# Tile 3 gathered instead of tile 6, and top-k scans taken into the query projections

## The chip, the cores and the metric

The kernel runs on one core of a Trainium2 chip. The metric is the device time of one execution in microseconds; a kernel's time is the median of its runs. TensorE (PE in the profile) multiplies matrices, VectorE is DVE, ScalarE is ACT, GpSimd is POOL, and SP is the queue that issues most transfers.

## The reference

One encoder layer on 1024 tokens of width 1024: a projection, forgetting attention (FoX) and RWKV-7 time mixing side by side, a gated merge, a layer norm, then PEER, a lookup of single-neuron experts, and a second layer norm. The change concerns PEER:

```python
q = (xb @ w_q).reshape(t, PEER_HEADS, 2, PEER_HALF)
s = jnp.einsum('thpd,hpkd->thpk', q, sub_keys).astype(jnp.float32)
top_s, top_i = lax.top_k(s, K)
cand_s = top_s[:, :, 0, :, None] + top_s[:, :, 1, None, :]
cand_i = top_i[:, :, 0, :, None] * PEER_N_KEYS + top_i[:, :, 1, None, :]
best_s, best_pos = lax.top_k(cand_s.reshape(t, PEER_HEADS, K * K), K)
idx = jnp.take_along_axis(cand_i.reshape(t, PEER_HEADS, K * K), best_pos, axis=-1)
gate = jax.nn.softmax(best_s, axis=-1).astype(xb.dtype)
h = jax.nn.gelu(jnp.einsum('thkd,td->thk', u_table[idx], xb), approximate=False)
return jnp.einsum('thk,thkd->td', gate * h, v_table[idx])
```

There are 8 heads with two sets of 128 sub-keys each (16 key sets), K is 16, so every token has 128 experts out of 16384. `u_table` and `v_table` are 16384 x 1024 float32.

## The kernel before

Tokens are cut into eight tiles of 128. The front works in two halves of 512 tokens (tiles 0 to 3, then 4 to 7): `fox`, `rwkv_half`, `merge_half`, and at the end of the merge `queries`, which computes the 16 projections and the scores of four tiles. Scores of four key sets at a time (a group) leave PSUM by an ACT copy and go to a DRAM tensor `scd`.

After the second half `dense_block` treats PEER in two ways. For the three tiles in `DENSE` (3, 4, 5) it computes the hidden values of all 16384 experts by matmul, in a loop of 128 steps of 128 experts over all of `u` and `v`; the gates enter through coefficients C, which a one-hot stage of 96 steps before the loop builds from each tile's selected indices (two one-hot matrices a token, multiplied on TensorE; part of C stays in SBUF, part goes to DRAM as `cd` and comes back). The five tiles in `GATHERED` (0, 1, 2, 6, 7) fetch only their chosen rows: 128 key rows a tile (one row of `u` for each of the 128 tokens, 128 x 1024 float32), by an indirect DMA on GpSimd and a product with a sum on VectorE (`experts_in`), and then 128 value rows a tile from `v`, by indirect DMA and small matmuls (`Rows`, tile `pg`; a step takes two rows).

Two background queues run beside the main code. `g.B` holds generators of top-ks (`topk`) and key rows (`experts_in`); `g.V` holds the value rows. Every matmul issued by `mm` pays both queues its priced length in us times a rate (`RATEP` by stage of the front, fox, RWKV, merge with queries; `RATEB` and `RATEV` in the one-hot stage and in the loop), and a queue runs steps until its credit is spent. Each `yield` names the step's cost: 1.46 for a key row, 0.5 for half a key set of a scan, 3 for a value step. While one queue runs, matmuls pay it nothing. `mix` interleaves two generators by weights (`TKW`). A generator that yields None has nothing to do yet and gives its credit up.

`topk` waits until its tile's scores are all written, reloads them group by group, scans each key set (five VectorE operations: the largest eight, replaced, the next eight, and two index searches), adds candidates, scans those, and turns ranks into expert indices with one-hot products. Its results go to DRAM (`seld`, `cijd`, `gated`).

The order of `g.B` before: the top-k of tile 0; the rows of tiles 0, 1 and 2, each mixed with the top-k of the next tile; the top-ks of 4, 5 and 6; the rows of 6 mixed with the top-k of 7; the rows of 7. So when the one-hot stage begins, tile 3 has long been selected (`selections` asks for it with `need`), and the value rows start at the same time.

In the front only TensorE's order is that of the program; in `dense_block` also those of GpSimd and VectorE, so there an instruction that waits holds up all behind it on its engine. Key rows land in places of 128 x 1024: five in the first half, two more in the second (`KRING`), parts of C in the loop. The value rows have a ring of seven and the parts of C not yet written.

Of the kernel before, what the change touches and what calls it, by code (L numbers as in the profile page):

```python
# [22 lines left out]
LATER = 0  # L23
BLEAD = 3
KRING = (5, 2)
TKW = (45.0, 56.25, 59.895)
TKI = 1
RATEP = (1, 1, 0.9)

RATEB = (2.1, 0.46)  # L30
RATEV = (4.2, 0.52, 1.25)
SEL = (1, 2, 3)
DENSE = (3, 4, 5)
GATHERED = (0, 1, 2, 6, 7)
LATE = (4, 5, 6)

RING = 7

# [362 lines left out]
def body(ctx, g):  # L401
# [34 lines left out]

    g.rank = g.tk.tile([128, 16, 16], BF16, name="rank")
    dve.tensor_copy(g.rank, g.iota[:, 0:16, None].to_broadcast([128, 16, 16]))
    g.scored = set()
    g.B.add(topk(g, 0), "k0")  # L440
    for k, t in enumerate(SEL):
        g.B.add(mix(experts_in(g, k), 190.0, g.B.tagged(topk(g, t), f"k{t}"), TKW[k]), f"g{k}")
    for t in LATE:
        g.B.add(topk(g, t), f"k{t}")
    g.B.add(mix(experts_in(g, 6), 190.0, g.B.tagged(topk(g, 7), "k7"), TKW[2]), "g6")
    g.B.add(experts_in(g, 7), "g7")
    if g.stop:
        g.B.q = []

# [66 lines left out]
def front_setup(g, fe, order):  # L516
    tc, nc, A = g.tc, g.nc, g.A
    dve, act, sp = g.dve, g.act, g.sp
    fp = fe.enter_context(tc.tile_pool(name="fe", bufs=1))
    g.wp = fe.enter_context(tc.tile_pool(name="wp", bufs=1))  # L520
    g.W = Weights(g, order, len(order) // len(PARTS))
    tab = fp.tile([128, TAB.shape[1]], F32, name="tab")

    def tb(name, rows=slice(0, 128)):
        o, n = TAB_OFF[name]
        return tab[rows, o:o + n]

    g.tb = tb
    yield
    sp.dma_start(tab, A["tab"])  # L530
    g.rst = fp.tile([128, 512], BF16, name="rst")
    dve.memset(g.rst, 1.0)
    dve.memset(g.rst.rearrange("p (c t) -> p c t", t=64)[:, :, 0:1], 0.0)
    g.vec = vec = fp.tile([128, N_VEC], F32, name="vec")
    sp.dma_start(vec, A["vec"])
    g.omu = fp.tile([128, 14], F32, name="omu")
    dve.tensor_scalar(g.omu, vec[:, V_MU:V_MU + 14], -1.0, 1.0, op0=OP.mult, op1=OP.add)

    g.oka = fp.tile([128, 4], F32, name="oka")
    dve.tensor_scalar(g.oka, vec[:, V_KA:V_KA + 4], -1.0, 1.0, op0=OP.mult, op1=OP.add)  # L540
    g.prev = fp.tile([128, 14], F32, name="prev")
    dve.memset(g.prev, 0.0)
    g.sigma = fp.tile([128, 4, 2, 64], F32, name="sigma")
    dve.memset(g.sigma, 0.0)
    g.ck = fp.tile([128, T], F32R, name="ck")
    dve.memset(g.ck.bitcast(F32), 0.0)
    g.ccar = fp.tile([8, 1], F32, name="ccar")
    dve.memset(g.ccar, 0.0)
    yield


def fox(g, hf, X):
# [7 lines left out]
    with ExitStack() as fx:  # L560
# [98 lines left out]
        def chunks(ct, e, P_, yu, su, vc):  # L659
# [32 lines left out]
            if e:  # L692
                dve.reciprocal(su, su)
                pr = psT.tile([128, n], F32, name="pt")
                for qi in range(nq):
                    pe.transpose(pr[0:2, qi * 128:(qi + 1) * 128], su[:, qi, :], ident)
                ri = sm.tile([2, n], F32, name="ri", bufs=1)
                act.copy(ri, pr[0:2, :])
                yield
                pr = psT.tile([128, n], F32, name="pt")  # L700
                mm(g, pr, tb("sel2", slice(0, 2)), ri, True, True)
                dve.tensor_mul(yu, yu, pr)
                act.dma_start(g.yfd[ct * 128:(ct + 1) * 128, cols], yu)
                yield
# [550 lines left out]
def queries(g, hf, x1, rest, ps_):  # L1255
# [5 lines left out]
    with ExitStack() as fx:  # L1261
# [13 lines left out]
        def scores(gr, q):  # L1275
            for tt in range(n // 128):
                ps = ps_.tile([128, 4, 128], F32, name=f"o{tt}", bufs=2)
                for j in range(4):
                    mm(g, ps[:, j, :], q[:, j, tt * 128:(tt + 1) * 128], sk[:, 4 * gr + j, :], True, True)
                sc = qp.tile([128, 512], F32, name="sc", bufs=2)  # L1280
                act.copy(sc, ps.rearrange("p a b -> p (a b)"))
                sp.dma_start(g.scd[tt0 + tt][:, gr * 512:(gr + 1) * 512], sc)

        last = None
        for gr in range(4):
# [16 lines left out]
            g.scored.add(tt0 + tt)  # L1302


def topk(g, tile_):

    dve, act, sp = g.dve, g.act, g.sp
    while tile_ not in g.scored:
        yield None
    P = g.tk  # L1310
    tv = P.tile([128, 16, 16], F32, name="tv")
    ti = P.tile([128, 16, 16], U32, name="ti")
    def load(gr):
        sc = P.tile([128, 4, 128], F32, name="s", bufs=2)
        sp.dma_start(sc, g.scd[tile_][:, gr * 512:(gr + 1) * 512].rearrange("p (a b) -> p a b", a=4))
        return sc

    nxt = load(0)
    yield 1.0
    yield 1.0  # L1320
    for gr in range(4):
        sc = nxt
        if gr < 3:
            nxt = load(gr + 1)
        for j in range(0, 4, TKI):
            ii = range(4 * gr + j, 4 * gr + j + TKI)
            tmp = P.tile([128, 2, 128], F32, name="tmp")
            for i in ii:
                dve.max(tv[:, i, 0:8], sc[:, i % 4, :])
            for i in ii:  # L1330
                dve.match_replace(tmp[:, i % 2, :], tv[:, i, 0:8], sc[:, i % 4, :], NEG)
            for i in ii:
                dve.max(tv[:, i, 8:16], tmp[:, i % 2, :])
            yield 0.5 * TKI
            for i in ii:
                dve.max_index(ti[:, i, 0:8], tv[:, i, 0:8], sc[:, i % 4, :])
            for i in ii:
                dve.max_index(ti[:, i, 8:16], tv[:, i, 8:16], tmp[:, i % 2, :])
            yield 0.5 * TKI
    v4 = tv.rearrange("p (h s) k -> p h s k", s=2)  # L1340
    cand = P.tile([128, 8, NCAND], F32, name="cand")
    for a_, (n, o) in enumerate(zip(CAND, CAND_OFF)):
# [110 lines left out]
def dense_block(g, C):  # L1453
# [59 lines left out]
        return a, b  # L1513

    g.B.rate, g.V.rate = RATEB[0], RATEV[0]
    zx = ExitStack()
    xt = None
    n4 = n // 4
# [374 lines left out]
```

## Time and profile before

| | us |
|---|---|
| median of 3 runs | 3609.86 |
| lowest, highest run | 3596.46, 3627.01 |
| the profiled execution | 3587.89 |
| its span, first to last instruction | 3586.1 |
| mean granted TensorE clock | 0.938 |

The profile is of one execution. Times in it are us from the first instruction. A group or a stretch lists the busy time of an engine with the number of its instructions in brackets; the clock is the share of TensorE's full clock that was granted, and the DMA share is the mean busy share of the core's 16 DMA engines. A wait is put down to what ended it.

### The profile page before, as it was taken

What the parts mean: (1) busy time and instruction counts of PE and PEld (TensorE: products, weight loads), DVE (VectorE), ACT (ScalarE), POOL (GpSimd) and SP (SyncE); (2) the same over time, 40 slices, a digit from 0 to 9 for tenths busy, and PEclk for the clock granted to TensorE, in tenths of its full rate; (3) what the DMA queues carried; (4) which work ended last, traced back from release to release, by engine and by line L of the source; (5) the groups of instructions that cost most, each with busy time, mean ns of one, the idle gap of its engine ahead of it and who ended that gap; (6) DMA issues with size and microseconds to landing.
All of it is one profiled execution on the core that took longest, in us unless ns stands there. A gap on an engine that the chain in (4) does not pass through costs nothing. (4 is left out here: it accounts for less than half of the span.)

```text
span 3586.1 us, 55687 instructions
## 1 busy us (share of the span) xinstructions
PE 3156.2 (88%) x20656; PEld 2304.5 (64%) x20656; DVE 2263.6 (63%) x5118; ACT 1165.6 (33%) x2453; POOL 2071.5 (58%) x1686
## 2 busy tenths in 40 slices
PE   7899998999987778878767777999999999999997
PEld 5577776775566566557533323887777777776665
DVE  2235423359988997886478854777766767763324
ACT  3443222333432121201244433334333433333332
POOL 2032114415565565644365566888887888886773
PEclk9999998999998988899888888999999999999998
DMA  6373257878888888999698999999999999999995
GB/s 234 112 246 116 95 180 246 294 282 299 298 342 310 288 295 322 357 363 392 248 376 341 351 369 380 363 361 358 383 396 372 403 374 398 399 382 341 389 394 191
DMA packets 369377, 1133.15 MB, mean 316 GB/s; under 512 B 49744, under 2 KB 88400, under 8 KB 367312
## 3 DMA queue, kind: packets, MB, share of 16 engines
q0 software_dynamic: 184320, 671.17, 49.1%
q1 hardware_dynamic: 172672, 437.64, 33.8%
q10 hardware_dynamic: 12112, 20.78, 1.6%
q8 instruction: 162, 2.65, 0.3%
q14 instruction: 111, 0.91, 0.1%
HBM read 999.87 MB, written 129.56 MB: 315 GB/s over the span
## 5 line engine op out<-in xcount | busy, mean ns | idle before, releaser
L1429 POOL DMA_INDIRECT g<-u,eidx x566 | 696.9, 1231 | 448.3 <-DVE hh L1435 156.8
L1435 DVE CUSTOM_DVE_ANT_0 g<-g,ext 128x1024 f32<-128x1024 f32 x566 | 728.5, 1297 | 70.3 <-DMA g<-u,eidx 64.3
L1731 POOL DMA_INDIRECT vr<-v,ve x434 | 457.8, 1055 | 196.3 <-issue 104.1
L291 POOL TENSOR_TENSOR wl<-wraw,wh 128x1024 fp32r<-128x1024 f32 x65 | 157.1, 2416 | 439.9 <-ACT wh L290 334.3
L273 PE MATMUL pg<-vr,win 128*32 128x512 f32 x1736 | 311.9, 636 | 65.4 <-DMA vr<-v,ve 62.3
L273 PE MATMUL b<-xh,uh 128*128 128x384 f32 x1024 | 350.7, 342 | 14.2 <-DVE C L1616 13.0
L273 PE MATMUL b<-xh,ul 128*128 128x384 f32 x1024 | 352.2, 344 | 8.0 <-POOL ul L291 7.9
L273 PE MATMUL b<-xl,uh 128*128 128x384 f32 x1024 | 349.5, 341 | 0.0
L273 PE MATMUL v<-vl,ch 128*128 128x512 f32 x768 | 305.9, 398 | 12.8 <-POOL vl L291 12.7
L273 PE MATMUL v<-vh,ch 128*128 128x512 f32 x768 | 302.9, 394 | 0.0
L273 PE MATMUL v<-vh,cl 128*128 128x512 f32 x768 | 301.7, 393 | 0.0
L273 PE MATMUL pj<-xh,wh 128*128 128x512 f32 x624 | 281.9, 452 | 19.2 <-ACT xh L290 7.6
L290 ACT CAST uh<-uraw 128x512 fp32r<-128x512 f32 x256 | 158.6, 620 | 365.2 <-PE b L273 267.5
L1731 POOL DMA_INDIRECT C<-v,ve x206 | 215.0, 1044 | 90.2 <-issue 47.4
L273 PE MATMUL pj<-xl,wh 128*128 128x512 f32 x624 | 257.0, 412 | 1.9 <-DVE xl L291 1.9
L273 PE MATMUL pj<-xh,wl 128*128 128x512 f32 x624 | 255.7, 410 | 0.0
L291 DVE TENSOR_TENSOR vl<-vraw,vh 128x512 fp32r<-128x512 f32 x128 | 134.6, 1051 | 178.3 <-ACT vh L290 110.9
L290 ACT CAST vh<-vraw 128x512 fp32r<-128x512 f32 x256 | 158.2, 620 | 252.2 <-PE v L273 174.9
L273 PEld LDWEIGHTS v<-ab 128*128 128x128 f32 x768 | 112.1, 216 | 182.6 <-issue 107.4
L291 POOL TENSOR_TENSOR ul<-uraw,uh 128x512 fp32r<-128x512 f32 x128 | 171.3, 1338 | 88.6 <-ACT uh L290 73.3
L273 PEld LDWEIGHTS b<-xh,uh 128*128 128x128 f32 x1024 | 194.3, 190 | 35.1 <-DVE C L1616 15.5
L273 PEld LDWEIGHTS b<-xh,ul 128*128 128x128 f32 x1024 | 194.3, 190 | 34.9 <-issue 24.3
(357 smaller groups left out, 6598.0 us busy)
## 6 DMA issues: line engine op xcount, KB each, us to landing
uraw<-ut SPq DMA_DIRECT2D x128, 512.0 KB
vraw<-vt SPq DMA_DIRECT2D x128, 512.0 KB
wraw<-w SPq DMA_DIRECT2D x75, 512.0 KB
wh<-whd SPq DMA_DIRECT2D x75, 512.0 KB
wl<-whd SPq DMA_DIRECT2D x75, 512.0 KB
whd<-wh SPq DMA_DIRECT2D x71, 512.0 KB
whd<-wl SPq DMA_DIRECT2D x71, 512.0 KB
cd<-S SPq DMA_DIRECT2D x12, 1344.0 KB
```

What stands on the lines that cost most here:

```text
L273: g.pe.matmul(o, l, r, start=start, stop=stop_)
L290: g.act.copy(hi, src)
L291: (lo_eng or g.dve).tensor_sub(lo, src, hi.bitcast(F32))
L1429: pool.indirect_dma_start(out=place, out_offset=None, in_=A["u"], in_offset=bass.IndirectOffsetOnAxis(ap=idx[:, n:n + 1], axis=0))
L1435: dve.tensor_tensor_reduce(out=gg, in0=gg, in1=xt, scale=1.0, scalar=0.0, op0=OP.mult, op1=OP.add, accum_out=hh[:, k:k + 1])
L1731: g.pool.indirect_dma_start(out=place, out_offset=None, in_=g.A["v"], in_offset=bass.IndirectOffsetOnAxis(ap=self.meta[i][1][:, t:t + 1], ...
```

## The change

Tile 3 moves from `DENSE` to `GATHERED` and tile 6 the other way. The rows of tile 3 stand last in the front's queue, mixed with scans of three score groups. A new function `scans` takes scores that are still in SBUF and scans them without a reload: in the first half all four groups of tile 0 and three groups each of tiles 1 and 2 (ten scans, kept in key places, which are free then), in the second half three groups of tile 4, the first dense tile. These groups are not written to `scd`, and `topk` begins behind them. At the start of `dense_block` a new loop steps the top-k of tile 4 to its end, two background steps for each value step, before any one-hot work. Then the rest of tile 3's rows is mixed with the top-ks of 5, 6 and 7 at weights 1 to 2, followed by the rows of tile 7. The rates change. A small tile `ri` in `fox` shares the buffers of `th`.

```diff
-TKW = (45.0, 56.25, 59.895)
+TKW = (31.0, 38.8, 56.25)
+EARLY = (0, 1, 2)
 TKI = 1
-RATEP = (1, 1, 0.9)
-
-RATEB = (2.1, 0.46)
-RATEV = (4.2, 0.52, 1.25)
+RATEP = (1, 1, 1.15)
+
+RATEB = (2.1, 0.32)
+RATEV = (3.5, 0.555, 0.88)
 SEL = (1, 2, 3)
-DENSE = (3, 4, 5)
-GATHERED = (0, 1, 2, 6, 7)
-LATE = (4, 5, 6)
+DENSE = (4, 5, 6)
+GATHERED = (0, 1, 2, 3, 7)
...
-    g.scored = set()
+    g.scored, g.fresh, g.tops = set(), [], {}
+    g.B.add(scans(g, 3 * len(EARLY) + 1))
     g.B.add(topk(g, 0), "k0")
     for k, t in enumerate(SEL):
         g.B.add(mix(experts_in(g, k), 190.0, g.B.tagged(topk(g, t), f"k{t}"), TKW[k]), f"g{k}")
-    for t in LATE:
-        g.B.add(topk(g, t), f"k{t}")
-    g.B.add(mix(experts_in(g, 6), 190.0, g.B.tagged(topk(g, 7), "k7"), TKW[2]), "g6")
-    g.B.add(experts_in(g, 7), "g7")
+    g.B.add(mix(g.B.tagged(experts_in(g, 3), "g3"), 1.0, scans(g, 3), 1.0), "s3")
...
-                ri = sm.tile([2, n], F32, name="ri", bufs=1)
+                ri = sm.tile([128, n], F32, name="th", bufs=4)[0:2, :]
...
-                sc = qp.tile([128, 512], F32, name="sc", bufs=2)
+                if hf == 0:
+                    near = tt in EARLY and (gr < 3 or tt == 0)
+                    k = (3 * gr + tt) % 9 if near else 9 if gr < 3 or tt == 1 else tt - 1
+                    sc = g.keys.all[k // 2][:, k % 2 * 512:k % 2 * 512 + 512]
+                else:
+                    near = tt0 + tt == DENSE[0] and gr < 3
+                    sc = qp.tile([128, 512], F32, name="sf", bufs=3) if near else qp.tile([128, 512], F32, name="sc", bufs=4)
                 act.copy(sc, ps.rearrange("p a b -> p (a b)"))
-                sp.dma_start(g.scd[tt0 + tt][:, gr * 512:(gr + 1) * 512], sc)
+                if near:
+                    g.fresh.append((tt0 + tt, gr, sc.rearrange("p (a b) -> p a b", a=4)))
+                else:
+                    sp.dma_start(g.scd[tt0 + tt][:, gr * 512:(gr + 1) * 512], sc)
...
+def scan(g, tv, ti, gr, sc):
+
+    dve = g.dve
+    for i in range(4 * gr, 4 * gr + 4):
+        tmp = g.tk.tile([128, 2, 128], F32, name="tmp")[:, i % 2, :]
+        dve.max(tv[:, i, 0:8], sc[:, i % 4, :])
+        dve.match_replace(tmp, tv[:, i, 0:8], sc[:, i % 4, :], NEG)
+        dve.max(tv[:, i, 8:16], tmp)
+        yield 0.5
+        dve.max_index(ti[:, i, 0:8], tv[:, i, 0:8], sc[:, i % 4, :])
+        dve.max_index(ti[:, i, 8:16], tv[:, i, 8:16], tmp)
+        yield 0.5
+
+
+def scans(g, n):
+
+    for _ in range(n):
+        while not g.fresh:
+            yield None
+        t, gr, sc = g.fresh.pop(0)
+        if t not in g.tops:
+            g.tops[t] = tops(g)
+        yield from scan(g, *g.tops[t], gr, sc)
...
-    nxt = load(0)
-    yield 1.0
-    yield 1.0
-    for gr in range(4):
+    grs = range(4)
+    if tile_ in g.tops:
+        tv, ti = g.tops[tile_]
+        grs = range(3 + (tile_ == 0), 4)
+    else:
+        tv, ti = tops(g)
+    if grs:
+        nxt = load(grs[0])
+        yield 1.0
+        yield 1.0
+    for gr in grs:
         sc = nxt
...
     g.B.rate, g.V.rate = RATEB[0], RATEV[0]
+    rest, tags = g.B.q.pop(0)
+    assert tags == ("s3",) and not g.B.q
+    g.B.add(topk(g, tiles[0]), f"k{tiles[0]}")
+    g.B.add(mix(rest, 1.0, chain([g.B.tagged(topk(g, t), f"k{t}") for t in (5, 6, 7)]), 2.0))
+    g.B.add(experts_in(g, 7), "g7")
+    g.B.busy = g.V.busy = True
+    while f"k{tiles[0]}" not in g.B.done:
+        for a in (g.B, g.B, g.V):
+            a._step()
+    g.B.busy = g.V.busy = False
```

More of the change, by code (lines that the diff above doesn't have):

```diff
@@ L519, in front_setup @@
     fp = fe.enter_context(tc.tile_pool(name="fe", bufs=1))
+    g.tops[0] = tops(g)
+    for t in EARLY[1:]:
+        g.tops[t] = fp.tile([128, 16, 16], F32, name=f"tv{t}"), fp.tile([128, 16, 16], U32, name=f"ti{t}")
     g.wp = fe.enter_context(tc.tile_pool(name="wp", bufs=1))
@@ L1302, in queries, with tops @@
             g.scored.add(tt0 + tt)
+def tops(g):
+    return g.tk.tile([128, 16, 16], F32, name="tv"), g.tk.tile([128, 16, 16], U32, name="ti")
+def scan(g, tv, ti, gr, sc):
[17 more added lines that the diff above has]
+        yield from scan(g, *g.tops[t], gr, sc)
 def topk(g, tile_):
@@ L1310, in topk @@
     P = g.tk
-    tv = P.tile([128, 16, 16], F32, name="tv")
-    ti = P.tile([128, 16, 16], U32, name="ti")
     def load(gr):
@@ L1316, in load @@
         return sc
-    nxt = load(0)
-    yield 1.0
-    yield 1.0
-    for gr in range(4):
-        sc = nxt
[L1323 to L1339, printed above, removed]
+    grs = range(4)
[9 more added lines that the diff above has]
+    for gr in grs:
+        sc = nxt
+        for i, c in enumerate(scan(g, tv, ti, gr, sc)):
+            yield c
+            if gr < 3 and i == 3:
+                nxt = load(gr + 1)
     v4 = tv.rearrange("p (h s) k -> p h s k", s=2)
```

## The prediction

> **What bounds the kernel now.** I read the page first (busy shares and the 40 slices), then the table by stage that the stretches view gives, then the same stretches for the key-row line and for the value-row tile, and last the waits of TensorE stage by stage.
>
> ```profile
> PE 3156.2 (88%) x20656; PEld 2304.5 (64%) x20656; DVE 2263.6 (63%) x5118; ACT 1165.6 (33%) x2453; POOL 2071.5 (58%) x1686
> ...
> PE   7899998999987778878767777999999999999997
> ...
> DMA  6373257878888888999698999999999999999995
> ```
>
> TensorE is busy for 88% of the span, and what is missing lies in the middle slices, where its digits fall to 7 and 6. The DMA digits are 8 and 9 in nearly all slices from the eleventh on, so transfers are the second candidate. The stages tell which it is where. The columns after the length are busy time of PE, PEld, DVE, ACT and POOL, the granted clock, the DMA share, and GB/s.
>
> ```profile
> 690.00:756.00 66.00, 66.00 (x341) 56.46 (x340) 9.00 (x7) 25.70 (x39) 22.25 (x11) 1.00 0.85 310
> 756.00:1480.00 724.00, 618.10 (x5175) 438.82 (x5173) 644.78 (x1740) 202.22 (x349) 392.31 (x316) 0.91 0.85 309
> 1480.00:1756.00 276.00, 221.64 (x996) 176.49 (x996) 197.53 (x427) 40.85 (x68) 132.83 (x108) 0.90 0.92 356
> 1756.00:1780.00 24.00, 5.82 (x29) 5.23 (x30) 13.61 (x58) 9.27 (x29) 3.48 (x4) 0.61 0.20 63
> 1780.00:2212.00 432.00, 313.66 (x1681) 137.28 (x1680) 313.52 (x1311) 168.72 (x558) 266.69 (x256) 0.86 0.95 364
> 2212.00:3266.00 1054.00, 1019.66 (x5433) 813.52 (x5434) 724.03 (x1062) 387.57 (x781) 872.58 (x713) 0.99 1.00 380
> 3266.00:3558.00 292.00, 283.47 (x1589) 198.48 (x1588) 81.76 (x109) 97.87 (x222) 191.90 (x180) 0.99 0.92 347
> ```
>
> The stages are: the end of the first queries (to 756), fox and RWKV of the second half (to 1480), its merge and queries (to 1756), a gap (to 1780), the one-hot stage that builds the coefficients C (to 2212), and the dense loop of 128 steps, with key rows in flight until 3266 and without them to 3558. TensorE idles 106, 54, 18, 118, 34 and 9 us in the last six. Only the one-hot stage has a large gap in TensorE together with a DMA share near 1; the loop has a full DMA share too, but TensorE hardly waits in it.
>
> ```profile
> PE s L273 <- DVE x L981: 31.6, 19, 4.3
> ...
> PE o L273 <- DMA wh<-whd: 18.4, 4, 9.2
> PE o L273 <- DMA wl<-whd: 10.6, 7, 2.1
> ...
> PE pg L273 <- DMA vr<-v,ve: 60.2, 36, 12.1
> PE v L273 <- ACT S L1556: 28.7, 10, 6.5
> ...
> PE v L273 <- POOL vl L291: 12.7, 16, 2.2
> PE b L273 <- DVE C L1616: 11.5, 3, 6.2
> PE b L273 <- POOL ul L291: 7.9, 6, 2.4
> ```
>
> These are TensorE's waits (total us, times, longest) in four stages, in order. In RWKV it waits for VectorE; in the merge and queries for weights, 29 us; in the one-hot stage for value rows, 60 us; in the loop for VectorE and GpSimd, 32 us over 1054.
>
> **The change part by part.** It moves background work; the count of dense matmuls, value rows and key rows stays the same. So I first count where each row goes, then price the places.
>
> ```profile
> 756.00:1480.00 724.00, 349.90 (x571) 0.91 0.85 309
> 1480.00:1756.00 276.00, 125.94 (x198) 0.90 0.92 356
> ...
> 1780.00:2212.00 432.00, 32.93 (x54) 0.86 0.95 364
> 2212.00:3266.00 1054.00, 330.28 (x458) 0.99 1.00 380
> ```
>
> This is line L1435, the key-row products, in the same stretches: two instructions a row, so 285, 99, 27 and 229 rows. A row costs VectorE 1.23 us in the second half (349.90/285.5) and 1.44 us in the loop (330.28/229).
>
> *Credits.* The background queue is paid per matmul by the code's own price times a rate. Adding those prices for the second half gives 187 for fox, 379 for RWKV and 178 for merge and queries. Before, at rates 1, 1 and 0.9, that is 725 credits; the queue asks 3 x 191 for three tiles of rows and 4 x 38.6 for four top-ks, 727. The trace bears the count out: the last row of tile 2 is multiplied at 1738.7, just before the queries end.
>
> ```profile
> 1738.73 0.08 DVE L1435 DVE_READ_ACCUMULATOR2_ANT hh<- 128x1 f32 x1
> 1762.85 1.12 DVE L1506 TENSOR_SCALAR ab<-base,cT 128x128 f32<-128x128 f32 x4 [24.04 <-ACT cT L1497]
> ```
>
> After, the last rate is 1.15, so there are 770 credits. Ten scans and their loads (42 credits) have gone to the first queries; what stays of four top-ks and three tiles is 687, three scans of tile 4 take 12, and about 70 are left: 46 rows of tile 3 (1.46 credits each). The code prices the 384 one-hot matmuls at 82 us, which at rate 2.1 is 172 credits as before: the top-ks of tiles 5, 6 and 7 (116) and 38 rows of tile 3. Some 44 rows are left for the loop, with 128 of tile 7: about 170 in place of 229.
>
> *Scans in the first queries.* Their VectorE cost is read from the first top-k before.
>
> ```profile
> 760.72 0.49 DVE L1329 MAX8 tv<-s 128x8 f32<-128x128 f32 x2 [21.99 <-DMA s<-scd]
> ...
> 771.07 0.29 DVE L1338 FIND_INDEX8 ti<-tv,tmp 128x8 uint32<-128x128 f32 x1
> ...
> 792.22 2.24 DVE L1343 TENSOR_TENSOR cand<-tv 128x64 f32<-128x64 f32 x1
> ...
> 821.77 0.23 DVE L1395 CAST idx<-t 128x128 int32<-128x128 f32 x1
> ```
>
> The rows from 760.72 to 771.36 hold eight key sets, two scans, so one scan is 5.3 us and ten are 53 us. VectorE idles 57 us of the 66 that end at 756, so they fit, but nearly fill it. What can be late is a split of weights or of the next x that stands behind a scan; TensorE is busy without a pause there. I take +1, between 0 and +5. Ten reloads and thirteen stores of scores of 0.26 MB fall away; the score copies lose their wait for a buffer, beside full matmuls: nothing.
>
> *Fox and RWKV of the second half.* VectorE loses 53 us of scans, gains 12 of tile 3's earlier top-k and 35 rows (42 credits and the scans' place) at 1.23, 43 us: even. The rows add 18 MB, 51 us at 364 GB/s, to a stage whose DMA share leaves 15% of 724 us, 109 us. I take 0, from -8 (rows start some 25 us earlier, when VectorE waited 22 us for scores) to +8.
>
> *Merge and queries of the second half.* At 204 credits instead of 160 there are about 121 rows instead of 99, 11.5 MB more, and three scans. That is 32 us of DMA where 8% of 276 us, 22 us, is free: +10. VectorE goes from 198 to about 230 of 276 us, and rows that wait for their data hold up the products and sums behind them. I take +11, from 0 (the tail after 1738 was free) to +30 (all of the transfer shows). The Trainium skill (DMA: Bandwidth & Descriptors, section Queues, rings and completion order) says that a DMA engine takes turns between its queue rows packet by packet; by that rule the weight queue keeps about half of the engines however many rows are queued, the weights would not become much later than the 29 us of waits shown, and with this term near 0 instead of +11 the sum would be -17 and the forecast 3593. No row of the run before separates the two.
>
> *The gap and the one-hot stage.* Before, the first dense tile (3) was chosen long ahead. Now it is tile 4, whose last scan, candidates, ranks and gates must come after the last scores. That is one reload, a scan of 5.3 us, and the stretch from 792.2 to 822.0 above, 30 us, plus a store and a reload of the selection.
>
> ```profile
> 1761.38 0.87 PE L1496 MATMUL v<-base,cij 128*128 128x128 f32 x3 [7.26 <-DMA cij<-cijd]
> 1764.62 4.46 PE L273 MATMUL v<-ab 128*128 128x128 f32 x22 [2.37 <-DVE ab L1512]
> ...
> 1779.84 1.88 PE L273 MATMUL pg<-vr,win 128*32 128x512 f32 x2 [10.43 <-DMA vr<-v,ve]
> ```
>
> The first one-hot matmul moves from 1764.6 to about 1806, 41 us. Up to seven rows of tile 3 that must be flushed stand ahead on VectorE: 9 us at the worst. Meanwhile the new loop emits one value step per two background steps: 37 steps of the top-k, 18 calls, of which four prepare, so 14 value steps on TensorE. They do not wait behind one-hots any more and start at about 1770 instead of 1779.8. In the one-hot stage proper the value rate falls from 4.2 to 3.5 on those 82 us, at 3 a step: from 112 steps counted to 96.
>
> ```profile
> 1780.00:2212.00 432.00, 187.18 (x896) 25.35 (x894) 1.76 (x3) 0.86 0.95 364
> 2212.00:3266.00 1054.00, 135.48 (x1104) 28.93 (x1104) 2.34 (x4) 0.99 1.00 380
> 3266.00:3558.00 292.00, 74.88 (x560) 15.75 (x560) 1.76 (x3) 0.99 0.92 347
> ...
> cd<-S SPq DMA_DIRECT2D x12, 1344.0 KB
> ```
>
> Value steps (tile pg, eight instructions each) were 112, 138 and 70. Whether the 41 us show hangs on what limits this stage. Its bytes: 224 value rows of 0.524 MB are 117 MB, 12 spills 16, 34 key rows with those in flight 18, the rest 6; 157 MB, and 432 us x 364 GB/s is 157. So it runs at the DMA's pace, and a later one-hot start is free as long as rows flow. After, gap and stage together move 220 value rows, 38 key rows and the same rest: 157 MB again, starting 10 to 12 us earlier. I take -12, from -25 to +41 (no overlap at all).
>
> *The loop.* 210 value steps instead of 208 at 0.98 us (135.48/138): +2. About 59 rows fewer on VectorE, GpSimd and the queues, of 229: the 32 us of waits go down by a quarter, -8. Nothing larger is to be had, since TensorE's own pace sets it.
>
> ```profile
> 3547.18 4.08 PE v L273 x18
> 3551.26 4.24 PE b L273 x24
> ```
>
> A step is 8.32 us at full clock; 128 of them and 208 value steps are 1269 us of the 1346, and part of the rest is the start of the loop. I take -6, from -25 to 0. After 3558 nothing changes: the norms of three dense tiles as before.
>
> *Sum:* +1 + 0 + 11 - 12 - 6 = -6 us. The profiled execution took 3587.89 us, which becomes 3582. It lies 22 us under the median of the runs shown (3609.86) and under the lowest of them, so the forecast for a median is 3604 us.
>
> **The rivals.**
>
> *The dense part is DMA-bound as a whole (faster).* From 1780 to 3266 the DMA share is 0.95 to 1.00. If that were the limit, the 46 rows that leave it (24 MB, 63 us at 380 GB/s), hidden in the free 15% of the second half, would show nearly whole: about 55 us, 3555. For it speaks the one-hot stage, where TensorE idles 118 us; against it the loop, where it idles 34 of 1054. It decides only if merge and queries swallow their rows.
>
> *The second half pays (slower).* Weight fetches and key rows share the engines; if the fetches fall behind at every one of the 16 query projections by 2 us, which is the longest single wait for wl now, and the merge's products queue behind rows, the stage grows by 32 + 13 = 45 us: 3655. For it speak 29 us of such waits already; against it that VectorE still has 78 us free there. It decides from a growth of the waits for whd over 50 us.
>
> *The gap shows (slower).* If the one-hot stage is limited by order on VectorE rather than by bytes, the 41 us come on top: 3604 + 12 + 41 = 3657. For it: the clock in the gap was 0.61, and the first two value matmuls there took 1.88 us, more than the 1.67 us of a mean step of eight (187.18/112). The Trainium skill (TensorE: Matmul & The Clock Gate, Part 1) says that an idle window of about 3.4 us puts TensorE on half clock; the 0.61 agrees. Against the rival: even at twice the mean the 14 value steps are 47 us, about the gap itself, and the bytes of the stage fit its length within 1%.
>
> *The rows do not come over.* If tile 2 is not done before the queries end, the scans of tile 4 fall after them too, and the gap grows by 16 us with nothing gained in the loop: some 3628. The credit count, right within 2 of 727, speaks against it.
>
> **How the numbers follow.** About 1%, 36 us, is what a measurement of this kernel can tell from no change: its three runs spread over 31 us. My forecast, terms that nearly cancel, has a chance of 0.53; the DMA-bound rival 0.25; the second half 0.10; the gap 0.08; rows that stay behind 0.04. The first and the last lie within 1%, with tails: faster 0.27, same 0.54, slower 0.19. The range from 3558 to 3646 leaves the ends of both sides out; the forecast's own range is 3575 to 3635.
>
> **What would show it.** Right: 90 to 100 key rows of tile 3 multiplied by the end of the one-hot stage, about half of them before the queries end; VectorE near 0.9 busy in the first queries with TensorE still full; first one-hot matmul about 50 us after the last score matmul, value rows ahead of it; the loop starting within 20 us of 2212 and lasting 1335 to 1346 us. Wrong: waits for whd above 50 us; TensorE idle over 30 us between the last score and the first value step; a one-hot stage of 430 us again; a loop under 1320 us.

## The result and the profile after

| | before | after |
|---|---|---|
| median of ten runs, us | 3605.2 | 3583.9 |
| lowest, highest | 3591.24, 3627.01 | 3570.19, 3598.23 |
| ratio after/before, 95% interval | | 0.9942 [0.9916, 0.9968] |
| profiled execution, us (span) | 3587.89 (3586.1) | 3598.23 (3596.5) |

The change is worth some 20 us, 0.6%, which is within 1%. The two profiled executions point the other way: the one of before lies 17 us below its median, and the one of after is the slowest of its ten. Whoever subtracts one span from the other finds a loss of 10 us that the medians don't have. So I compare the traces by stages, and later the same stages in further executions of the same two kernels.

The first view is the table of stretches of the changed kernel, with the columns as before (length; busy time of PE, PEld, DVE, ACT, POOL; clock; DMA share; GB/s).

```profile
700.00:765.00 65.00, 65.00 (x337) 55.64 (x336) 46.32 (x246) 25.99 (x40) 22.48 (x10) 1.00 0.82 283
765.00:1490.00 725.00, 620.16 (x5070) 439.61 (x5069) 634.69 (x1588) 189.45 (x331) 412.04 (x331) 0.87 0.86 311
1490.00:1778.00 288.00, 234.81 (x1102) 185.88 (x1100) 221.46 (x466) 49.37 (x82) 146.42 (x129) 0.91 0.98 375
1778.00:1818.00 40.00, 0.95 (x4) 0.58 (x5) 36.33 (x132) 2.55 (x8) 30.45 (x23) 0.51 0.90 325
1818.00:1870.00 52.00, 37.94 (x131) 5.20 (x131) 25.25 (x110) 9.11 (x27) 33.22 (x35) 0.85 0.99 370
1870.00:2272.00 402.00, 289.51 (x1572) 137.25 (x1572) 332.79 (x1310) 174.72 (x558) 258.28 (x238) 0.85 0.96 366
2272.00:3222.00 950.00, 940.53 (x5076) 748.48 (x5077) 521.55 (x721) 357.98 (x725) 741.05 (x621) 0.99 0.99 369
3222.00:3567.00 345.00, 345.00 (x1943) 258.93 (x1942) 96.60 (x142) 126.55 (x271) 214.24 (x200) 1.00 0.90 327
```

The rows are: the first queries, fox and RWKV of the second half, its merge and queries, a gap, value steps without one-hots, the one-hot stage, the loop with key rows, the loop without. Three things are new. The first queries have VectorE busy for 46 of 65 us where it was 9 of 66, and TensorE has no pause. TensorE stands still for a whole 40 us after the second queries, at a granted clock of 0.51, and VectorE is busy there. And the loop's first part is 950 us long instead of 1054, with TensorE idle for 9 us of it instead of 34.

Where the key rows went, by their product line in the same stretches (two instructions a row):

```profile
765.00:1490.00 725.00, 369.57 (x608) 0.87 0.86 311
1490.00:1778.00 288.00, 138.72 (x221) 0.91 0.98 375
1778.00:1818.00 40.00, 23.41 (x40) 0.51 0.90 325
...
1870.00:2272.00 402.00, 59.83 (x98) 0.85 0.96 366
2272.00:3222.00 950.00, 204.43 (x313) 0.99 0.99 369
```

By the end of the queries 414 rows are done, 384 of tiles 0 to 2 and 30 of tile 3. Twenty more fall into the gap, 49 into the one-hot stage, and 157 are left to the loop. Before, 27 rows lay between the queries and the loop; now 69 do.

The waits of the changed kernel (total us, times, longest): of VectorE from the merge to the end of the gap, then of TensorE in the merge and queries, in the gap and the value steps behind it, and in the loop while key rows run.

```profile
DVE g L1467 <- DMA g<-u,eidx: 54.1, 43, 11.0
...
PE o L273 <- DMA wl<-whd: 13.0, 9, 4.5
...
PE o L273 <- DMA wh<-whd: 6.8, 5, 3.2
...
PE pg L273 <- DMA vr<-v,ve: 45.4, 14, 37.9
...
PE b L273 <- DVE C L1658: 6.2, 1, 6.2
PE pg L273 <- DMA vr<-v,ve: 2.0, 4, 1.1
```

Merge and queries wait less for weights than before (19.8 us, not 29.0). VectorE waits 54 us for key rows, 11.0 of them in one piece. The first value matmul waits 38 us. In the loop the 32 us of waits for VectorE and GpSimd have shrunk to the single 6.2 us for C at its start.

The timeline shows what stands in the gap; the columns are start, duration, engine, instruction, and the wait in brackets.

```profile
1769.93 4.00 PE L273 MATMUL o<-sk,q 128*128 128x128 f32 x32
...
1803.51 1.23 DVE L1467 CUSTOM_DVE_ANT_0 g<-g,ext 128x1024 f32<-128x1024 f32 x1 [0.72 <-DMA g<-u,eidx]
1804.66 0.29 DVE L1325 MAX8 tv<-s 128x8 f32<-128x128 f32 x1
...
1813.10 0.23 DVE L1761 CAST ve<-vr 128x128 int32<-128x128 f32 x1
...
1817.95 1.89 PE L273 MATMUL pg<-vr,win 128*32 128x512 f32 x2 [37.88 <-DMA vr<-v,ve]
...
1867.39 0.55 PE L1528 MATMUL v<-base,cij 128*128 128x128 f32 x3
1870.26 0.49 PE L273 MATMUL v<-ab 128*128 128x128 f32 x2 [2.32 <-DVE ab L1544]
```

VectorE multiplies the rows that were asked for during the queries (one as late as 1803.5), and the scans of tile 4's last scores and the cast of the first value rows' indices (1813.1) stand behind them. So the last score, at 1773.7, and the first value matmul, at 1818.0, are 44 us apart, and the first one-hot comes 97 us after that score: ahead of it in TensorE's order stand 16 value steps, and the matmuls that prepare it (L1528) begin where these end, at 1867.4, without a wait.

One reason why the rows are late stands earlier in the same trace.

```profile
1706.64 0.94 POOL L1461 DMA_INDIRECT g<-u,eidx  x1 [20.24 <-DMA eidx<-seld]
...
1714.75 1.23 DVE L1467 CUSTOM_DVE_ANT_0 g<-g,ext 128x1024 f32<-128x1024 f32 x1 [10.99 <-DMA g<-u,eidx]
```

Between the last row of tile 2 and the first of tile 3, GpSimd fetches nothing for 20.2 us. The tile `eidx` has one buffer, which holds tile 2's indices and then its gates, until tile 2's products are multiplied by these (to 1699.2); the load of tile 3's indices is issued behind that, at 1699.4. VectorE waits 11.0 us for the first row of tile 3. The fetches that follow are 1.24 us apart, so by estimate 20.2 us are time for some 16 rows. All ten traces with the change's front have this wait, of 19.3 to 21.5 us; the traces with the old order of tiles have none from the merge to the gap. No run gave `eidx` a second buffer, so what it costs is not shown.

Cut at fixed events, the stages are (second half: from the last score of the first queries to the last of the second; gap and one-hot: from there to the first dense matmul; loop: from there to the last):

| us | start of the first queries | second half | gap and one-hot | loop |
|---|---|---|---|---|
| before | 691.2 | 988.3 | 457.3 | 1351.9 |
| after | 700.2 | 999.1 | 498.7 | 1300.8 |

The last two are large and nearly cancel: +41 and -51. The first two differ by 9 and 11 us. In the later runs the start lay between 688.1 and 699.1 us with the change's front and between 690.5 and 695.2 with the old one, and the second half scatters as much (table below), so these differences are those of one program from execution to execution.

### The profile page after: what moved, and what is told of

Read it like the earlier page. It is cut to its first block, busy times and chain, and to the rows that moved or that the text cites. A ratio compares the mean times of both kernels' runs of the same rounds, so it can differ in the third digit from the quotient of the medians.

```text
span 3596.5 us, 55631 instructions
## 1 busy us (share of the span) xinstructions
PE 3172.0 (88%) x20656; PEld 2315.6 (64%) x20656; DVE 2194.9 (61%) x5118; ACT 1170.0 (33%) x2450; POOL 2047.9 (57%) x1686
## 4 chain that ended last, share of the span: by engine, by line
PE 59%; DVE 16%; DMA 9%; issue 6%; POOL 3%; ACT 1%; another core or an unknown queue 0%; SPq 0%; ACTq 0%; POOLq 0%; DVEq 0%
PE v L273 16%; PE b L273 15%; PE pj L273 7%; PE pg L273 7%; DVE g L1467 5%; PE s L273 5%; DMA g<-u,eidx 3%; PE o L273 3%; DMA vr<-v,ve 2%; PE S L273 2%; POOL g L1461 2%; POOL vr L1773 1%; DVE ab L1538 1%; PE po L273 1%; PE pt L675 1%
## 5 line engine op out<-in xcount | busy, mean ns | idle before, releaser
L1461 POOL DMA_INDIRECT g<-u,eidx x592 | 705.0, 1191 | 456.4 <-DVE hh L1467 166.9
L273 PE MATMUL pg<-vr,win 128*32 128x512 f32 x1768 | 334.4, 632 | 84.6 <-DMA vr<-v,ve 74.2
L291 DVE TENSOR_TENSOR vl<-vraw,vh 128x512 fp32r<-128x512 f32 x128 | 126.4, 987 | 244.3 <-ACT vh L290 117.1
L1773 POOL DMA_INDIRECT C<-v,ve x198 | 206.7, 1044 | 80.9 <-issue 47.9
L291 POOL TENSOR_TENSOR vl<-vraw,vh 128x512 fp32r<-128x512 f32 x128 | 187.7, 1466 | 48.8 <-ACT vh L290 47.8
```

Of the source, the lines that this page charges most:

```text
L273: g.pe.matmul(o, l, r, start=start, stop=stop_)
L291: (lo_eng or g.dve).tensor_sub(lo, src, hi.bitcast(F32))
L1461: pool.indirect_dma_start(out=place, out_offset=None, in_=A["u"], in_offset=bass.IndirectOffsetOnAxis(ap=idx[:, n:n + 1], axis=0))
L1773: g.pool.indirect_dma_start(out=place, out_offset=None, in_=g.A["v"], in_offset=bass.IndirectOffsetOnAxis(ap=self.meta[i][1][:, t:t + 1], ...
```

## Experiments

All kernels are timed against the kernel before on the same chip; ratios are to it, with their 95% interval. A table of all the stages follows the last experiment.

**The changed kernel once more, without an edit.**

> The changed kernel unaltered, for a second profile, since its first one fell on the slowest of ten runs. If the stage lengths are properties of the program: end of the second queries to the first value matmul about 40 us idle, one-hot stage about 400 us, loop about 1295 us, and the rest of the difference between the two profiles lies in the first half and the RWKV stage. If they are scatter of one run, the loop comes out near the 1347 us of before and the idle time near 26.

3595.18 us against 3606.26, ratio 0.9965 [0.9946, 0.9983]. Its stages are 999.8, 493.3 and 1302.9 us: gap and one-hot +36, loop -49. Both shifts come back; the gain is somewhat smaller.

**Before, with fewer key rows in the loop.** Theory: the loop is shorter because fewer rows share its DMA and engines. This kernel leaves out 72 key rows of tile 6, whose hidden values are set to zero; the rate keeps rows flowing to the same place of the loop as after.

```diff
-RATEB = (2.1, 0.46)
-RATEV = (4.2, 0.52, 1.25)
+RATEB = (2.1, 0.36)
+RATEV = (4.2, 0.555, 0.88)
...
-    for k in range(128):
-        while n < 128 and len(keys.free) > 1:
+    rows = 56 if tile_ == 6 else 128
+    if rows < 128:
+        dve.memset(hh[:, rows:128], 0.0)
+    for k in range(rows):
+        while n < rows and len(keys.free) > 1:
```

> The kernel before, with 72 key rows of tile 6 left out (their products are set to zero) and the loop's rates set so that key rows end at about the same step as in the changed kernel; all before the loop as before. Theory A (the loop gets shorter because fewer key rows run beside it): loop about 1295 to 1305 us instead of 1347, total about 45 us under before. Theory B (the loop got shorter through something else in the change, such as the order of tiles or what is resident): loop stays at 1335 to 1350 us, total within 10 us of before.

3579.7 us, ratio 0.9918 [0.9894, 0.9942]. The loop takes 1323.1 us, 29 less than before, with 158 rows in it, and so lies between the two figures set against each other. The stretch with rows, and the one behind them:

```profile
2228.00:3171.60 943.60, 926.80 (x5005) 738.20 (x5006) 571.69 (x885) 359.37 (x722) 734.86 (x615) 0.99 0.98 368
3171.60:3551.00 379.40, 369.95 (x2041) 275.02 (x2040) 100.22 (x150) 133.69 (x283) 221.75 (x208) 0.99 0.86 308
```

Fewer and thinner rows, with the value rates set as in the diff, bring 29 of the 51 us. VectorE still has 885 instructions here where the changed kernel has 721. The groups of the kernel before in its own loop (count | busy us, mean ns | idle before) show what they are:

```profile
L1375 DVE TENSOR_TENSOR rb<-rb,t 128x128 bf16<-128x128 bf16 x8 | 4.0, 495 | 0.3
...
L1356 DVE MAX8 bs<-tmp 128x8 f32<-128x50 f32 x8 | 1.7, 214 | 0.3
```

These are candidates and ranks of the top-k of tile 7, mixed there with the rows of tile 6. In the loop of the changed kernel no such group is left: its top-ks are all done before the loop begins. That is a part of the change which the prediction didn't see. Taking the row products out, VectorE's work while rows run is 358 us here (571.69 - 213.50) and 317 us after (521.55 - 204.43). It is a candidate for a part of the other 22 us of the loop, but hardly for all: behind the last key row, where no top-k runs, TensorE idles 9 us here (379.40 - 369.95) and 0 after (345.00 of 345.00). Most of these 9 us are a value row that came 7 us late. While rows run TensorE idles 17 us here and 9 after, and in the whole loop it is busy for 1297 us here and 1292 after. That leaves some 13 us for the top-k, and no run moved it alone: its share is argued and not shown.

**After, with the rows of the loop as dense as before.** Same 157 rows, but at the old rate, so that they crowd into the loop's first 700 us.

```diff
-RATEB = (2.1, 0.32)
+RATEB = (2.1, 0.46)
```

> The changed kernel with the loop's key-row rate put back to 0.46, so the same 157 rows come as densely as in the kernel before and end at step 70 instead of 94. If the density of rows per us makes the waits in the loop, they come back while rows run: 20 to 35 us of TensorE idle and a loop of 1320 to 1330 us, total 25 us above the changed kernel. If only the number of rows counts, the loop stays within 8 us of 1295.

3621.13 us, ratio 1.0044 [1.0027, 1.0062]. The loop takes 1331.1 us, 30 more than after, and the waits come back. Stretch, then waits in it:

```profile
2266.00:2965.60 699.60, 669.22 (x3549) 523.66 (x3550) 444.94 (x607) 250.74 (x510) 581.04 (x481) 0.98 1.00 385
```

```profile
PE b L273 <- POOL ul L291: 12.5, 7, 3.1
PE v L273 <- POOL vl L291: 9.1, 12, 2.2
PE pg L273 <- DMA vr<-v,ve: 5.4, 2, 4.9
```

So it isn't the number of rows alone: 157 rows in 700 us (224 per ms, 385 GB/s) idle TensorE for 30 us, and in 950 us (165 per ms, 369 GB/s) for 9. Before had 217 per ms at 380 GB/s and 34 us. The names of the waits say GpSimd (`ul` and `vl`), but its split of `u` stands behind ScalarE's cast of the same weights. In the dense run that cast waits nine times for the weights to land, 30.8 us in all, and in the changed kernel once:

```profile
ACT uh L290 <- DMA uraw<-ut: 30.8, 9, 5.0
...
ACT uh L290 <- DMA uraw<-ut: 2.0, 1, 2.0
```

So with dense rows the weights arrive late. In the kernel before, the same wait is 12.4 us, less than its 34 us of idle TensorE, so there it is not the whole cause. The DMA stands at 1.00 in both dense cases and at 0.99 with fewer GB/s in the thin one.

**After, with the old price in merge and queries.** Theory: with fewer rows asked for there, VectorE has no backlog at the end of the queries.

```diff
-RATEP = (1, 1, 1.15)
-RATEB = (2.1, 0.32)
+RATEP = (1, 1, 0.9)
+RATEB = (2.1, 0.42)
```

> The changed kernel with the merge and query rate at 0.9 as before (about 30 rows of tile 3 fewer in the second half) and the loop's rate at 0.42 so that all rows still end in time. If VectorE falls behind in the queries because more rows are asked for than the DMA brings, the backlog is gone: the first value matmul comes within 20 us of the last score matmul instead of 44, merge and queries are 5 to 10 us shorter, the loop 10 to 20 us longer, total within 10 us of the changed kernel. If the gap comes from the chain of the top-k itself, it stays at 40 us or more.

3603.8 us, ratio 0.9983 [0.9960, 1.0007]. The first value matmul comes 20 us after the last score (44 after the change), the first one-hot 73 us (97), and gap and one-hot take 475.2 us, 18 to 24 less than in the two runs of the changed kernel. The loop gets 186 rows and takes 1326.3 us, 24 more. Gain and loss cancel; the second half was also 16 us longer, for which I have no cause. The profiled execution is the slowest of its ten, 8 us over their median.

**Before, with the ten early scans alone.** The edit is the change's `scans`, `scan` and `tops` for the first half, with its buffers for `sc` and `ri`; split, order and rates of before, and no early scans in the second half.

```diff
+EARLY = (0, 1, 2)
+    g.B.add(scans(g, 3 * len(EARLY) + 1))
...
+                else:
+                    near = False
```

> The kernel before with only the ten scans in the first queries (split of the tiles, queue order and rates as before). If those scans are the gain, the total is 15 us or more under before. If the gain is the row count in the loop, which this kernel does not change, the loop stays at about 1350, gap and one-hot stage at 457, and the total within 8 us of before; what can change is the second half, by up to -10 us.

3570.66 us against 3563.57 on this chip, ratio 1.0015 [0.9995, 1.0036]. The scans alone bring nothing. Their place in the first queries lasts 74.4 us from first to last score, as in every kernel (74.3 before). On this chip the one-hot stage is shorter than in the first profile of before:

```profile
1787.00:2191.00 404.00, 317.15 (x1678) 134.49 (x1676) 312.25 (x1307) 171.31 (x557) 263.74 (x254) 0.92 1.00 389
```

404 us x 389 GB/s is 157 MB, as 432 us x 364 was. For the same program that has to be so: length times mean rate gives the bytes whatever sets the pace. What differs is the DMA share, 1.00 here and 0.95 there. Divided by it the rates are 389 and 383 GB/s, so most of the 28 us are pauses of the DMA on the first chip. Why it paused there, no run shows.

**After, with the queue held back at the end of the queries.** The rate drops to 0.5 from the second score group of the second half on, and the loop's rate makes up for it.

```diff
-RATEB = (2.1, 0.32)
+RATEB = (2.1, 0.37)
...
+            if hf and gr == 1:
+                g.B.rate = 0.5
```

> The changed kernel with the background rate at 0.5 for the last two groups of the second queries (about 20 rows of tile 3 fewer asked for there, the backlog of VectorE) and the loop's rate at 0.37 so that they end in time. If the backlog is what delays the value rows and the first one-hot, the first value matmul comes about 20 us after the last score matmul instead of 44 and gap with one-hot stage is 470 to 475 us instead of 495, as in the run at rate 0.9; the loop grows by 5 to 15 us with 175 to 180 rows; total 5 to 20 us under the changed kernel. If it is not, gap and stage stay at 490 or more.

3543.12 us, ratio 0.9942 [0.9920, 0.9963]. The first value matmul comes 19 us after the last score, the first one-hot 70 us. The gap, and the value steps and one-hots behind it:

```profile
1751.00:1770.00 19.00, 1.24 (x11) 0.87 (x10) 16.24 (x96) 2.90 (x9) 6.08 (x8) 0.63 0.59 205
1770.00:2201.00 431.00, 316.86 (x1703) 136.91 (x1703) 356.38 (x1420) 187.67 (x584) 292.19 (x273) 0.90 0.99 385
```

The 20 rows that had stood in the gap are now in the loop, 178 there instead of 157.

**After, with fewer value steps in the one-hot stage**, and the same together with the hold.

```diff
-RATEV = (3.5, 0.555, 0.88)
+RATEV = (2.8, 0.64, 1.0)
```

> The changed kernel with the value rate of the one-hot stage at 2.8 instead of 3.5 (19 value steps, 20 MB, move from it to the loop, whose value rates go up to 0.64 and 1.0). If transfers pace gap and one-hot stage, they shrink from 495 us by 20 MB at 366 GB/s, 55 us, to about 440. If the order of VectorE and TensorE paces them, they shrink by less than 25. The loop grows by 19 steps at about 1.1 us, 20 us, to about 1322, or more if its transfers fill up. Total 0 to 30 us under the changed kernel.

> Both edits together: value rate 2.8 in the one-hot stage and background rate 0.5 late in the second queries. If gap and one-hot stage go at the pace of their bytes, both reductions add up: about 415 to 425 us. The loop has about 178 rows and 19 value steps more, 1330 to 1345 us. Total 10 to 40 us under the changed kernel, unless the loop's transfers fill up, in which case it stays level with it.

The first took 3594.55 us, ratio 1.0087 [1.0059, 1.0115], the second (hold, with a last rate of 1.1) 3566.78, ratio 1.0006 [0.9986, 1.0027]. Both are losses against the variant without the edit (the changed kernel has 0.9978 on the last chip, the hold 0.9942 on this one). Nineteen value steps went into the loop, 20 us of TensorE at 1.04, but the loop grew to 1356.5 and 1351.0 us, 58 and 42 more than in the same kernels without the edit, with TensorE idle for 20 and 27 us while key rows run (1322 us and 1330 to 1345 us had been expected). And gap and one-hot of the first shrank by less than their bytes: 19 steps of two rows are 20 MB, 51 us at 389 GB/s, and the stage fell from 472.6 (the changed kernel on the next chip, below) to 457.8 us. With the hold it fell by 16, from 449.9 to 433.7. Under 25 was the bound set for a stage paced by the order of VectorE and TensorE. From the first value matmul on, the first kernel shows this stretch and this wait:

```profile
1792.00:2204.00 412.00, 281.50 (x1551) 139.04 (x1549) 355.18 (x1418) 185.55 (x564) 252.57 (x235) 0.84 0.93 353
...
PE v L273 <- DVE ab L1544: 51.0, 18, 18.6
```

The DMA share fell to 0.93, VectorE is busy for 355 of 412 us, and TensorE waits 51 us for the `ab` that VectorE makes for the one-hots, where it waits 25 us in the changed kernel on the next chip. So bytes alone don't pace this stage: when they are taken away, VectorE's work holds it.

**Before, after, and two held versions side by side on one chip.** The last one adds to the hold a slower value rate while key rows run in the loop and a faster one behind them.

```diff
-RATEB = (2.1, 0.32)
-RATEV = (3.5, 0.555, 0.88)
+RATEB = (2.1, 0.37)
+RATEV = (3.5, 0.51, 1.1)
```

> The kernel before unaltered, so that its stages are read on the same chip as those of the next three. Ratio 1 within 0.002. Gap with one-hot stage between 429 and 457 us, the two lengths that two chips gave for the same program, at 157 MB over its transfer rate; loop 1350 to 1353 us whatever the chip, since its pace is set by waits while key rows run at rate 0.46.

> The changed kernel unaltered on the same chip. Loop 1301 to 1303 us, 50 us under before; gap and one-hot stage 35 to 41 us above before, of which the backlog of about 20 rows makes 20 to 25; last score matmul up to 12 us later than before. Ratio 0.994 to 0.997.

> The run that held key rows back late in the second queries, repeated beside the changed kernel on one chip. If the backlog costs what it seems to, gap and one-hot stage are 18 to 25 us shorter than in the changed kernel, the loop 5 to 10 us longer, the total 10 to 20 us under it: ratio to before 0.989 to 0.993. If the loop pays it all back, the two are level.

> The same with the loop's value rate at 0.51 while key rows run and 1.1 afterwards, so that value rows make room for the denser key rows. If the sum of bytes asked for per us is what brings waits into the loop, the demand while key rows run falls back to that of the changed kernel and TensorE's idle time there from 18 to below 10 us: total 0 to 10 us under the run before. If VectorE and GpSimd make the waits, nothing changes within 3 us.

Against 3566.7 us (27 runs of before): before itself 0.9993 [0.9976, 1.0011], after 3560.39 us, 0.9978 [0.9959, 0.9998], hold 3544.29 us, 0.9941 [0.9923, 0.9958], hold with the new value rates 3536.11 us, 0.9919 [0.9898, 0.9941]. The last beats both kernels; from after it is 24 us. After and the hold lie just outside the ratios expected (0.994 to 0.997 and 0.989 to 0.993). With the new value rates TensorE's idle time while key rows run falls from 20 to 15 us, not below 10, and the loop by 8, more than the 3 that were the bound if VectorE and GpSimd made the waits. So bytes have a part in them, and not the whole. Gap and one-hot of before, then of after, on this chip:

```profile
1760.00:1787.00 27.00, 6.60 (x37) 5.83 (x36) 13.62 (x58) 10.38 (x30) 3.75 (x4) 0.65 0.23 77
1787.00:2194.00 407.00, 324.57 (x1678) 133.49 (x1676) 312.85 (x1307) 171.35 (x558) 264.98 (x254) 0.92 0.99 386
```

```profile
1760.00:1805.00 45.00, 1.11 (x9) 0.71 (x7) 39.86 (x133) 2.92 (x9) 34.07 (x27) 0.54 0.90 327
1805.00:1857.00 52.00, 38.47 (x146) 6.71 (x147) 28.36 (x125) 12.09 (x33) 36.30 (x37) 0.93 1.01 392
1857.00:2233.00 376.00, 277.48 (x1560) 128.02 (x1559) 329.40 (x1302) 175.05 (x553) 262.20 (x236) 0.90 0.99 389
```

Length times rate gives 2.1 + 157.1 = 159 MB before and 14.7 + 20.4 + 146.3 = 181 MB after. The difference, 22 MB, is 42 key rows of 0.524 MB: 69 rows there instead of 27. At 389 GB/s 22 MB are 57 us. Before left some 21 us of transfers unused in its gap (27 us at 77 GB/s), after leaves 7; 57 - 14 is 43 us, and 39 were measured. This is an account and not a test, since the bytes come from length times rate. Cut at the first value matmul, the 39 us are 19 in the gap (45.1 instead of 26.2) and 20 from there to the loop (427.5 instead of 407.2). The hold takes away the first part and leaves the second: 18.9 and 427.3.

| us | second half | gap and one-hot | loop | key rows in the loop | TensorE idle while they run |
|---|---|---|---|---|---|
| before | 988.3 | 457.3 | 1351.9 | 229 | 34 |
| after | 999.1 | 498.7 | 1300.8 | 157 | 9 |
| after once more | 999.8 | 493.3 | 1302.9 | 157 | 9 |
| before, fewer rows | 1000.4 | 458.0 | 1323.1 | 158 | 17 |
| after, dense rows | 997.1 | 499.4 | 1331.1 | 157 | 30 |
| after, old price | 1015.6 | 475.2 | 1326.3 | 186 | 29 |
| before, scans alone | 997.2 | 428.8 | 1352.8 | 229 | 37 |
| after, fewer value steps | 984.1 | 457.8 | 1356.5 | 157 | 20 |
| after, hold | 984.8 | 449.9 | 1309.5 | 178 | 18 |
| after, hold, fewer value steps | 988.7 | 433.7 | 1351.0 | 178 | 27 |
| before, last chip | 995.8 | 433.4 | 1348.0 | 229 | 35 |
| after, last chip | 992.8 | 472.6 | 1298.3 | 157 | 10 |
| hold, last chip | 987.1 | 446.2 | 1314.5 | 178 | 20 |
| hold and new value rates, last chip | 995.0 | 445.0 | 1306.0 | 178 | 15 |

Rows 1 to 6 are from chips on which before takes some 3606 us, the others from chips on which it takes some 3565, so columns are compared within these two blocks. Each row is one execution; the farthest from its kernel's median are before (17 us under), after (14 over) and after with fewer value steps (13 under).

## Why the prediction was right and wrong

The time was within its range and its class, 20 us below the figure. Of these, 5 us lie in the base: the three runs that the forecast started from had a median of 3609.86, the ten have 3605.2. The sum of terms, -6 us, is near the -10 that the two stage pairs give for the part from the last score on (+41 - 51, and on the last chip +39 - 50). But two terms were wrong by 44 to 53 us each, in opposite directions, so that the sum came out right is luck. The rest of the 21 us between the medians shows in no stage; with one profiled execution of each kernel it can't be placed.

*First queries, +1: right.* The score stage lasts as long as before. VectorE came to 0.71 busy there, not 0.9.

*Fox and RWKV 0, merge and queries +11: the second term didn't come.* Before and the variant of it with fewer rows show 988.3, 995.8 and 1000.4 us for the second half, mean 994.8. The five kernels that have the change's front unaltered show 984.1, 992.8, 997.1, 999.1 and 999.8, mean 994.6. Within the first block of the table the change's front is 4 us longer in the mean, within the second 7 us shorter. The +11 of the first pair is within the scatter of one program. The queue of rows did grow: the DMA share went from 0.92 to 0.98, and VectorE's wait for rows from 38 us (the row of before is below) to 54, the gap's included; but 11.0 of the 16 us more are the one wait at the switch to tile 3. The weights paid nothing for the longer queue: waits for them went from 29.0 to 19.8 us, and on the last chip from 28.9 to 19.4. The rule of the Trainium skill that the prediction held against its own term (DMA: Bandwidth & Descriptors, section Queues, rings and completion order: a DMA engine takes turns between its queues packet by packet) agrees with these waits, though no run tests it by itself.

```profile
DVE g L1435 <- DMA g<-u,eidx: 38.1, 38, 2.8
```

*Gap and one-hot stage, -12: wrong, +36 to +41.* What failed is the step "157 MB again". It counted 46 rows of tile 3 as finished by the end of the queries, because the credits paid for that many. The credits were right, 50 had been asked for, but only 30 were multiplied: 304 rows in fox and RWKV and 110 in merge and queries, 414 where 430 had been counted. From the merge to the last score VectorE stands still for 50 us because rows are late, 11.0 of them in one piece at the switch of tiles. The prediction had allowed for seven rows to be flushed, 9 us at the worst; there were 20, and they took most of the gap. The one-hot stage then held 49 rows and not 38 (why not 38, I did not follow up), so 69 lay in the two together, 31 more than counted: 16 MB, 44 us at 366 GB/s. With that the term is -12 + 44 = +32.

The reason given, that the stage goes at the DMA's pace, holds only in part. That the bytes fitted its length "within 1%" was no evidence, since 364 GB/s was itself bytes over length. The DMA share speaks for it (0.95 in the first profile, 0.99 and 1.00 on the two later chips), the run with 20 MB less against it: 15 us came of 51, under the bound for a pace set by order. What bytes and order each contribute to the 20 us behind the gap is open.

The order in time was wrong too. The 99 rows of tile 3 by the end of the one-hot stage fit the sign of 90 to 100 (the sum's own counts, 46 and 38, make 84), but 30 instead of half of them came before the end of the queries. The first one-hot was to come about 50 us after the last score; it came after 97, and after 70 with the hold, because the 16 value steps ahead of it in TensorE's order take some 50 us from the first value matmul on. Two of the signs that were named against the prediction came: TensorE idle for over 30 us between the last score and the first value step (44), and a loop under 1320 us. The hold shows what the backlog is worth: gap and one-hot lose 26 us on the last chip (472.6 to 446.2), all of them in the gap, the loop gives back 16 with the rows that it gets for it, the second half is 6 us shorter, which its scatter covers, and the time falls by 16.

*The loop, -6: wrong, -50.* Value steps +2 was right within 2 (208 in both), and the 157 rows were near the 170 forecast. What failed is the sentence that nothing larger than a quarter of the 32 us of listed waits was to be had, "since TensorE's own pace sets it". By the stretches that it showed, TensorE was idle for 34 + 9 = 43 us of the 1346, and the pace of 1269 us left 77 unexplained. After, in 950 + 345 us, it idles for 9.5 us and is busy for 1286 us instead of 1303 with the same matmuls (whose ends the profile models). So of the 51 us 33 are idle time, most of what there was, and 18 are matmuls that took longer before. The two runs that changed the rows show 29 and 30 us for their thinning: fewer rows on the kernel before, and denser rows on the kernel after. The waits don't shrink in proportion to the rows: TensorE's idle time while they run went from 34 to 9 us as 229 rows became 157 thin ones, and back to 30 when the same 157 stood as dense as before. Of the other 22 us, 9 lie behind the last key row; the rest may go with the top-k of tile 7, which left the loop. That is open, as no run moved it by itself.

*The rivals.* The one that held the dense part as a whole to be DMA-bound had a part of the loop's mechanism: the dense run's waits for `uraw` and the run with new value rates point to transfers. Its price was too high, since of the 46 rows that were to leave the dense part only 30 did, and the gap ate most of what they freed. The rival of the gap that shows was right about the place and the 41 us, the figure partly by chance: the first one-hot came not 41 but 86 us later after the last score than before (97 and 11). It took VectorE's order for the alternative to a byte limit, and the runs show something of both.

## What to carry to other kernels

A queue that is paid in credits says when work is asked for and not when it is done. Where a stage begins with something that must come at once, look in the trace for what the in-order engine still has in front of it, and stop paying shortly before (here the hold, 16 us).

When TensorE is 97% busy and the DMA share is 1.00, the listed waits are a poor measure of what thinning the background work can bring: here 32 us were listed, and 51 came with the whole change. Work out TensorE's pace from undisturbed steps and explain the whole difference before calling a stage bound by it. And don't take length times mean rate for a test of a byte limit; take bytes away and see whether the stage shrinks by their time (here 15 us of 51).

A forecast near zero in which large effects may cancel should be checked stage by stage; here the right total hid two errors of 44 to 53 us.

## What the hardware showed that I hadn't expected

The same program took 3605 and 3606 us (medians of ten and twenty runs) in two sessions, and 3563.6 and 3566.7 us (23 and 27 runs) on two other chips, 1.1% less. Between the profiles of before (spans of 3586.1 and 3565.1 us) the difference is 21 us, and gap and one-hot stage alone are 24 us shorter; the loop, at 380 GB/s on both, differs by 4. The one-hot stage moved 386 instead of 364 GB/s at a DMA share of 0.99 instead of 0.95. Divided by the share these are 390 and 383 GB/s, so the busy DMA was nearly as fast on both, and most of the difference is pauses. TensorE waited 28.7 us for ScalarE's `S` in this stage on the first chip and 6.8 on the other; what makes the pauses is not shown. The change was 0.9942, 0.9965 and 0.9978 in three sessions. The intervals overlap, so a dependence on the chip isn't shown, but a gain of 0.6% and one of 0.2% are both what a single session of this change gives.
